# A SwiGLU stage on one core: a corner's sums, the weight sums, the stores and two matmul quarters change places

## The chip, the cores and the metric

The kernel runs on one core of one Trainium2 chip. The metric is the device time of one execution in microseconds (us); lower is better. The core's engines run side by side, each working through its own instructions in order: PE (TensorE, matrix products), DVE (VectorE), ACT (ScalarE), POOL (GpSimd) and SP, which issues transfers (DMA). An engine waits for another by a semaphore, and everything behind the waiting instruction on that engine waits too. Matrix products land in PSUM banks; other data is in SBUF.

## The reference

One transformer block over 1024 tokens of width 1024 in fp32. The change concerns its last part, the feed-forward layer (D_FF is 2816):

```python
h2 = rmsnorm(x, norm2_g[layer])
gate = jnp.einsum('bsd,df->bsf', h2, w_gate[layer])
up = jnp.einsum('bsd,df->bsf', h2, w_up[layer])
x = x + jnp.einsum('bsf,fd->bsd', jax.nn.silu(gate) * up, w_down[layer])
...
return rmsnorm(x, final_g)
```

Ahead of it stand a normed input projection, attention in 8 heads, a pooling mixer and an output projection.

## The kernel before

**Precision.** An fp32 value is split in a high and a low fp32r part (`split`: ACT writes the high part, L120, and DVE the low one, L121). A product of two such values is three matmuls (`mm3`): high by high (L161), page high by block low (L162), page low by block high (L163). A split pair of weight tiles is called a page. Three page slots are used in turn, so page n can be written when the products of page n−3 are done.

**The gate/up stage** runs from about 440 to 853 us over `NG` = 11 pairs of 128-wide blocks of D_FF. Each pair is a 2x2 block product done with seven products instead of eight (Strassen and Winograd's scheme): P1 to P7. Four of them need sums of weight blocks, which POOL makes (`gu_sums`, L1091: s1 to s4; s3 feeds P7, s2 P6, s1 P5, s4 P3). A product is 24 matmuls of 128x512 in two halves, n = 0 and 1. It adds up in PSUM: banks c1 take P1, P6 and P5 one after the other, banks c3 take P7 and then P4. From pair 1 on P3, and from pair 3 (`BOTH`) on P2 as well, is split a second time into seven quarter products Q1 to Q7 of 6 matmuls of 128x256 (`fine_product`), whose results DVE adds to SBUF tiles (L1277). Their pages come in two parts, "a" (Q1, Q2, Q7, Q4) and "b" (Q5, Q3, Q6), and `fine_sums` (DVE, L1234) makes the sums for them in place. In the trace these quarters write to `fineA`, `fineB` and `fineC`.

In pairs 3 to 10 the order is P1, P7, P2 and P6 interleaved, P5, then P3 and P4 interleaved, and the tables `PIECES` and `PIECES2` say how. After P1, P6 and P5 ACT copies c1's banks to SBUF (`snap`, L1153). The four corners of the result are then

- h11: P1's snapshot with P2's quarters added, Silu on ACT (L1302), product on POOL (L1303);
- h22: from c3 after P5 (`corner`: sums on DVE, L1172 and L1174, Silu on ACT, L1173, product on POOL, L1175);
- h21: the same from c3 after P4;
- h12: P5's snapshot with P3's quarters added, Silu on ACT (L1308), product on DVE (L1310).

POOL makes four features f1 to f4 out of these (L1179). Seven tiles a pair, corners and features, are stored to DRAM (`spill`, ACT's queue, L1281).

**The down stage** (to the end) reads them back and multiplies them with the down weights by the same seven-product scheme, in four groups of pairs. `down_sum` (L1349) makes sums of weights, `down_page` splits them, and L1614 adds results.

**Order.** A scheduler places each engine's instructions by priority. Where the code says `tc.issue_after(x)`, the instruction comes behind x on its engine; `mark[...]` remembers the last instruction of a kind (the last matmul, page, high part, quarter add, sum).

Of the kernel before, what the change touches and what calls it, by code (L numbers as in the profile page):

```python
# [30 lines left out]
NG = NF // 2  # L31
# [14 lines left out]
def tile_kernel(  # L46
# [1033 lines left out]
    def gu_sums(j):  # L1080
        a11, a12, a21, a22 = gu_parts(j)
        s1, s2, s3, s4 = (xw_tile(f"s{i}", f"s{i}_{j}", (P, 2, 512)) for i in (1, 2, 3, 4))
        at = None
        todo = [
            (s1, a21, a22, ALU.add), (s2, s1, a11, ALU.subtract), (s3, a11, a21, ALU.subtract), (s4, a12, s2, ALU.subtract)
        ]
        if j >= BOTH:
            todo.insert(0, todo.pop(2))
        for out, in0, in1, op in todo:
            with tc.issue_after(at.ins) if at and j >= BOTH else ExitStack():  # L1090
                at = nc.gpsimd.tensor_tensor(out=out, in0=in0, in1=in1, op=op)  # L1091
# [62 lines left out]

    spills = []
    feats = {}

    def feature(j, name, key):
        t = feats[name] = wk_tile("h", RING, f"{name}_{j}")
        if key:  # L1160
            spills.append((hsd[key, j], t))
        return t

    def corner(j, name, key, src, to):

        h = feature(j, name, to)
        q = wk_tile("q" if key else "e2", 1, f"q{name}_{j}")
        if key is None:
            nc.scalar.activation(out=q, in_=banks[src, 0], func=AF.Silu)
            nc.vector.tensor_tensor(out=h, in0=banks[src, 1], in1=q, op=ALU.mult)  # L1170
        else:
            nc.vector.tensor_tensor(out=q, in0=banks[src, 0], in1=snaps[j, key, 0], op=ALU.add)  # L1172
            nc.scalar.activation(out=q, in_=q, func=AF.Silu)  # L1173
            mark[name, j] = nc.vector.tensor_tensor(out=h, in0=banks[src, 1], in1=snaps[j, key, 1], op=ALU.add)  # L1174
            nc.gpsimd.tensor_tensor(out=h, in0=h, in1=q, op=ALU.mult)  # L1175
# [79 lines left out]
    def fine_product(j, k, q, acc):  # L1255

        at = FINE_BANK[q]
        if q in ("Q1", "Q7", "Q2"):
            own = BANKS["c2", int(k == "P3")], 1
            fine_banks[at] = bank(f"fine{at}_{j}{k}", *(own if at == "C" else ("m", 2)))  # L1260
        ps = fine_banks[at][:, QTR[0]]
        wh, wl = fine[j, k, q]
        bh, bl = fine[BLOCK[k], q]
        for c in range(2):
            ws = slice(c * P, (c + 1) * P)
            mm3(
                ps, wh[:, ws], wl[:, ws], bh[:, c, :], bl[:, c, :],
                q in ("Q1", "Q7", "Q2") and c == 0, q in ("Q3", "Q4", "Q2") and c == 1, True,
            )
        n, h = FINE_TO[q]  # L1270
        out = acc[n][:, QTR[h]]
        with ExitStack() as order:
            if q != "Q1":
                order.enter_context(tc.issue_after(mark["add"].ins))
            if (k, q) == ("P2", "Q3"):
                order.enter_context(tc.issue_after(mark["page"].ins))
            mark["add"] = nc.vector.tensor_tensor(out=out, in0=ps, in1=out, op=ALU.add)  # L1277

    def spill(due, q=nc.scalar):
        for d, h in due:  # L1280
            q.dma_start(out=d, in_=h)  # L1281

    def h22_from(j):
        return "P5" if j else "P7"

    def after(j, k):
        if k in ("P1", "P6", "P5"):
            with tc.issue_after(mark["P3a"][1].ins) if k == "P5" and j >= BOTH else ExitStack():
# [10 lines left out]
        if k == "P2b":  # L1299
            acc = [snaps[j, "sP1", n] for n in range(2)]  # L1300
            with tc.issue_after(mark["hi"].ins):
                nc.scalar.activation(out=acc[0], in_=acc[0], func=AF.Silu)  # L1302
            nc.gpsimd.tensor_tensor(out=acc[1], in0=acc[1], in1=acc[0], op=ALU.mult)  # L1303
            feats["h11"] = acc[1]
            spills.append((hsd["P1", j], acc[1]))
        if k == "P3b":
            acc = [snaps[j, "sU4", n] for n in range(2)]
            nc.scalar.activation(out=acc[0], in_=acc[0], func=AF.Silu)  # L1308
# [3 lines left out]
        if k == ("P3b" if j else "P4"):  # L1312
            with tc.issue_after(mark["add"].ins) if j else ExitStack():
                corner(j, "h21", "sU2", "c3", "P2")
        if k in ("P3", "P3b"):
            feature_sum(j, "f1", "P5", "h12", "h22", ALU.add)
            feature_sum(j, "f2", "P6", "f1", "h11", ALU.subtract)
            feature_sum(j, "f3", "P7", "h11", "h12", ALU.subtract)
        if k == ("P3b" if j else "P4"):
# [6 lines left out]
    PAGES = (("t3h", "t3l", "t1h", "t1l"), ("b22h", "b22l", "t4h", "t4l"))  # L1326
    SUMS = dict(P5="t2h", P6="t2l", P7="b21h", P4="b21l")
# [17 lines left out]
    def down_sum(b, k):  # L1345
        a0, a1 = dict(P5=("b12", "P1"), P6=("P3", "P5"), P7=("P3", "b12"), P4=("P2", "P6"))[k]
        t = blk_tile(SUMS[k], [P, len(GROUPS[b]), 512], F32, f"sum{k}_{b}")
        eng = nc.gpsimd if (b, k) in ((0, "P7"), (0, "P4")) else nc.vector
        eng.tensor_tensor(out=t, in0=moving[b, a0], in1=moving[b, a1], op=ALU.subtract)  # L1349
        moving[b, k] = t  # L1350

# [32 lines left out]
    WINDOWS2 = {"P2a": (0, "P2", "P6"), "P6": (1, "P2", "P6"), "P2b": (2, "P2", "P6")}  # L1384
    WINDOWS3 = {"P3a": (0, "P3", "P4"), "P4": (1, "P3", "P4"), "P3b": (2, "P3", "P4")}
    window = {j: dict(WINDOWS3 if j else {}, **(WINDOWS2 if j >= BOTH else {})) for j in range(NG)}

    def next_page(j, k):
        if (j, k) not in pages:
# [4 lines left out]
        if j + 1 < NG:  # L1394
# [3 lines left out]
                gu_raw(j + 1, 1)  # L1398
            if k == ("P3b" if j else "P4"):
                operands[j + 1] = gu_sums(j + 1)  # L1400

    PACE = {(1, "P1"): 3, (1, "P2"): 3, (2, "P1"): 2, (2, "P2"): 2, (2, "P6"): 3, (2, "P7"): 3}
    waiting = []
    for i, (j, k) in enumerate(todo):
        if i + 2 < len(todo) and (j < BOTH or k != "P1"):
            with ExitStack() as order:
                if j >= BOTH and k == "P3b":
                    order.enter_context(tc.issue_after(mark["add"].ins))
# [10 lines left out]
                mark["P3a"] = mark["page"], mark["hi"]  # L1419
        waiting.append(spills[:])  # L1420
        spills.clear()
        while len(waiting) > (1 if j < BOTH else 3):
            with tc.issue_after(mark["hi"].ins):
                spill(waiting.pop(0))
        if i == 1:
            product(j, k, 0, (0, 1))
            with tc.issue_after(mark["turn", ORDER[-1]].ins):
# [58 lines left out]
    for tt in range(NT):  # L1486
        nc.sync.dma_start(out=x2[tt], in_=x2d[tt])
# [171 lines left out]
```

## Time and profile before

| | us |
| --- | --- |
| median of 3 runs (1078.88 to 1079.73) | 1079.56 |
| the profiled execution | 1080.41 |
| its span in the trace | 1078.6 |
| PE busy | 1032.6 |
| DVE, ACT, POOL busy | 766.0, 470.0, 403.4 |
| granted clock of PE, mean over the span | 0.994 of full |

PE is busy 96% of the span. A row of the timeline gives start, duration, engine, line, operation and output<-inputs; in brackets stands how long the engine sat idle before it and whose work ended that. Rows of the list of waits give the total, the number of times and the longest.

### The profile page before, as it was taken

To read this page: it belongs to the slowest core of one execution; us is meant where nothing else is said; L and a number is where in the kernel's file an instruction comes from. 1 tells how busy PE (TensorE), PEld (TensorE's weight loads), DVE (VectorE), ACT (ScalarE), POOL (GpSimd) and SP (SyncE) were. 2 spreads that over 40 slices of the span, in tenths; PEclk is the share of its full clock that TensorE was granted. 3 is DMA by queue.
4 is the path that set the end of the run, shared out by engine and by line. 5 is a ranking of instruction groups with operands and counts; after the bars stand their busy time and mean duration, and the time that the engine had idled before them with its cause. 6 is when DMAs were issued, how large, how long until landed. Compare 5 with 4: busy or idle time off the path is not lost. (4 is left out here: it accounts for less than half of the span.)

```text
span 1078.6 us, 15149 instructions
## 1 busy us (share of the span) xinstructions
PE 1032.6 (96%) x5428; PEld 881.0 (82%) x5428; DVE 766.0 (71%) x1224; ACT 470.0 (44%) x759; POOL 403.4 (37%) x316
## 2 busy tenths in 40 slices
PE   9999999999999999998898998998998989999997
PEld 8988888998888888887787787887887868888886
DVE  7465566676885598988657657556566789888787
ACT  7343465565673375334234233332333323433345
POOL 4440121223461150846443734734735430000035
PEclk9999999999999999999999999999999989999999
DMA  6224334144831352323042142142146763344424
GB/s 240 51 69 138 79 102 111 42 114 118 299 107 31 110 167 60 127 83 113 11 147 90 57 147 88 59 146 88 59 127 201 251 221 126 138 166 156 147 88 156
DMA packets 108859, 130.28 MB, mean 121 GB/s; under 512 B 8040, under 2 KB 71024, under 8 KB 108784
## 3 DMA queue, kind: packets, MB, share of 16 engines
q1 hardware_dynamic: 97216, 108.18, 32.1%
q10 hardware_dynamic: 10928, 19.42, 5.0%
q0 software_dynamic: 640, 1.71, 0.5%
q8 instruction: 43, 0.70, 0.3%
q14 instruction: 32, 0.26, 0.1%
HBM read 86.29 MB, written 33.03 MB: 111 GB/s over the span
## 5 line engine op out<-in xcount | busy, mean ns | idle before, releaser
L162 PE MATMUL d<-d,d 128*128 128x512 f32 (+1 forms) x308 | 120.9, 393 | 4.0 <-DVE d L121 4.0
L163 PE MATMUL d<-d,d 128*128 128x512 f32 (+1 forms) x308 | 120.2, 392 | 0.0
L629 POOL TENSOR_SCALAR p<-p,rr 128x128 f32<-128x128 f32 (+3 forms) x64 | 48.7, 766 | 177.1 <-DVE rr L628 130.7
L161 PE MATMUL d<-d,d 128*128 128x512 f32 x308 | 109.7, 392 | 0.9 <-ACT d L120 0.7
L120 ACT ACTIVATE d<-r_f 128x1536 fp32r<-128x1536 f32 (+1 forms) x28 | 38.7, 1383 | 116.9 <-PE d L162 115.7
L162 PEld LDWEIGHTS d<-d,d 128*128 128x128 f32 x308 | 58.6, 190 | 16.6 <-DVE d L121 4.5
L161 PEld LDWEIGHTS d<-d,d 128*128 128x128 f32 x308 | 58.1, 189 | 14.2 <-ACT d L120 1.7
L163 PEld LDWEIGHTS d<-d,d 128*128 128x128 f32 x308 | 58.7, 191 | 12.1
L1510 POOL TENSOR_SCALAR sse<-sse 128x1 f32<-128x1 f32 x7 | 3.5, 497 | 171.4 <-ACT junk L1506 171.2
L1175 POOL TENSOR_TENSOR h<-h,qh 128x512 f32<-128x512 f32 x25 | 47.5, 1899 | 45.0 <-ACT qh L1173 39.2
L626 ACT ACTIVATE p<-p,mn 128x128 f32<-128x128 f32 (+3 forms) x64 | 49.4, 773 | 32.2 <-DVE mn L620 29.4
L121 DVE TENSOR_TENSOR gu_P_l<-s,gu_P_h 128x1024 fp32r<-128x1024 f32 (+1 forms) x38 | 53.9, 1428 | 6.7 <-ACT gu_P_h L120 6.6
L648 DVE TENSOR_TENSOR tl<-tp,th 128x512 fp32r<-128x512 f32 (+1 forms) x80 | 49.5, 633 | 9.8 <-ACT th L647 8.8
L120 ACT ACTIVATE gu_P_h<-s 128x1024 fp32r<-128x1024 f32 (+1 forms) x38 | 36.5, 968 | 42.0 <-PE gu_P L162 33.4
L1614 DVE TENSOR_TENSOR x2f_s<-d,x2f_s 128x512 f32<-128x512 f32 x64 | 42.8, 685 | 13.6 <-PE d L163 13.6
L121 DVE TENSOR_TENSOR d<-r_f,d 128x1536 fp32r<-128x1536 f32 (+1 forms) x28 | 46.0, 1644 | 6.8 <-ACT d L120 6.8
L163 PE MATMUL qk<-hTh,l_qk 128*128 128x512 f32 x128 | 50.7, 396 | 0.0
L161 PE MATMUL qk<-hTh,h_qk 128*128 128x512 f32 x128 | 50.6, 395 | 0.0
L162 PE MATMUL qk<-hTl,h_qk 128*128 128x512 f32 x128 | 50.4, 394 | 0.0
L647 ACT ACTIVATE th<-tp 128x512 fp32r<-128x512 f32 (+1 forms) x80 | 42.4, 550 | 15.6 <-PE tp L643 12.7
L1153 ACT ACTIVATE sn_sU<-gu_P 128x512 f32<-128x512 f32 x44 | 26.0, 590 | 50.6 <-PE gu_P L163 25.0
L1303 POOL TENSOR_TENSOR sn_sP<-sn_sP,sn_sP 128x512 f32<-128x512 f32 x8 | 11.4, 1421 | 96.8 <-ACT sn_sP L1302 96.8
(1174 smaller groups left out, 3389.6 us busy)
## 6 DMA issues: line engine op xcount, KB each, us to landing
r_f<-hsdP SPq DMA_DIRECT2D x77, 256.0 KB
r<-in_w_gate_dram SPq DMA_DIRECT2D x44, 256.0 KB
r<-in_w_up_dram SPq DMA_DIRECT2D x44, 256.0 KB
r_wd<-in_w_down_dram SPq DMA_DIRECT2D x22, 512.0 KB
hsdP<-f ACTq DMA_DIRECT2D x40, 256.0 KB
s<-hi SPq DMA_DIRECT2D x64, 128.0 KB
hsdP<-h ACTq DMA_DIRECT2D x23, 256.0 KB
x<-in_x_dram SPq DMA_DIRECT2D x8, 512.0 KB
```

Source lines behind the costliest of these rows:

```text
L120: mark["hi"] = nc.scalar.activation(out=hi, in_=src, func=AF.Copy)
L121: return eng.tensor_tensor(out=lo, in0=src, in1=f32(hi), op=ALU.subtract)
L161: nc.tensor.matmul(ps, lh, rh, start=start, stop=False, **kw)
L162: nc.tensor.matmul(ps, lh, rl, start=False, stop=False, **kw)
L163: mark["mm"] = nc.tensor.matmul(ps, ll, rh, start=False, stop=stop, **kw)
L626: nc.scalar.activation(out=pr[:, :n], in_=pr[:, :n], func=AF.Exp, scale=-1.0, bias=mn, accum_out=rs)
L629: nc.gpsimd.tensor_scalar(out=pr[:, :n], in0=pr[:, :n], scalar1=rr, scalar2=1.0, op0=ALU.mult, op1=ALU.mult)
L647: nc.scalar.activation(out=th[:, :w], in_=tp[:, :w], func=AF.Copy)
L648: nc.vector.tensor_tensor(out=tl[:, :w], in0=tp[:, :w], in1=f32(th[:, :w]), op=ALU.subtract)
L1153: mark["snap"] = nc.scalar.activation(out=t, in_=banks["c1", n], func=AF.Copy)
L1175: nc.gpsimd.tensor_tensor(out=h, in0=h, in1=q, op=ALU.mult)
L1614: added = nc.vector.tensor_tensor(out=row, in0=ps, in1=row, op=ALU.add)
```

## The change

Nothing computed changes, except where a tile lies; the edits change who does what, and when.

1. **Second corner behind the fourth product.** h21's two sums on DVE move from behind Q3 of P3 to behind Q6's add, where P4 ends. Its first sum goes back into the snapshot `sU2` it reads instead of the tile `q`. Its product on POOL stands behind s4.
2. **Weight sums ahead.** POOL's order is s3, s1, s2, s4, then h22's and h21's products, then f1 to f4; h22's product was between s3 and s1. The features and h12 are written down at the next pair's P1.
3. **Quarters between halves.** Behind P4, Q5 of P3 comes at once, then half 0 of the next pair's P1, Q3, and half 1; before, 10 matmuls of P1 stood ahead of Q5 and the other 14 between Q5 and Q3. Whole products follow each other in the order of the program, so in pair 2 P6 comes ahead of P7. P2's part "b" sums are made early, and on DVE all three stand ahead of the quarter adds.
4. **Stores spread.** Of the seven stores of a pair, two (h11, h22) were issued together with P1's end of the next pair and five after P6's page; now two go at the next pair's P7, two at P3a (h21, f1), two at P4 (f2, f3) and one at P3b (f4).
5. **Start of down.** Group 0's four sums of weights all go to POOL in pair 10 (before, two on DVE at the transition, two on POOL), and the tiles for pages and sums trade places. h11's store in pair 10 goes by POOL's queue.

POOL at the boundary of pairs 6 and 7, before (`s_7` are sums of pair 7, `r_7` its raw weights, `h_6` and `f_6` corners and features of pair 6, `qh` and `sU` the factors):

```order
L1091 TENSOR_TENSOR s_7_7095<-r_7_7029,r_7_7050 128x1024
L1175 TENSOR_TENSOR h_6_7083<-h_6_7083,qh_6_7084 128x512
L1091 TENSOR_TENSOR s_7_7093<-r_7_7050 128x1024
L1091 TENSOR_TENSOR s_7_7094<-s_7_7093,r_7_7029 128x1024
L1091 TENSOR_TENSOR s_7_7096<-r_7_7029,s_7_7094 128x1024
L1175 TENSOR_TENSOR h_6_7188<-h_6_7188,qh_6_7189 128x512
L1179 TENSOR_TENSOR f_6_7194<-sn_sU_7081,h_6_7083 128x512
L1179 TENSOR_TENSOR f_6_7196<-f_6_7194,sn_sP_6898 128x512
```

and after:

```order
L1091 TENSOR_TENSOR s_7_7085<-r_7_7020,r_7_7053 128x1024
L1091 TENSOR_TENSOR s_7_7083<-r_7_7053 128x1024
L1091 TENSOR_TENSOR s_7_7084<-s_7_7083,r_7_7020 128x1024
L1091 TENSOR_TENSOR s_7_7086<-r_7_7020,s_7_7084 128x1024
L1181 TENSOR_TENSOR h_6_7074<-h_6_7074,qh_6_7075 128x512
L1181 TENSOR_TENSOR h_6_7169<-h_6_7169,sn_sU_7012 128x512
L1190 TENSOR_TENSOR f_6_7199<-sn_sU_7072,h_6_7074 128x512
L1190 TENSOR_TENSOR f_6_7200<-f_6_7199,sn_sP_6897 128x512
```

Behind s3 h22's product has gone from its place ahead of s1 to one behind s4, next to h21's.

DVE at the same place, before (`fineA_6P` is the bank of Q5 and Q3, `gu_P_6909` and `gu_P_6922` the two c3 banks):

```order
L1277 TENSOR_TENSOR sn_sU_7081<-fineA_6P_7101,sn_sU_7081 128x256 x2
L121 TENSOR_TENSOR gu_P_l<-s_7_7095,gu_P_h 128x1024
L1234 TENSOR_TENSOR r_7_7029<-r_7_7029 128x256
L1277 TENSOR_TENSOR sn_sU_7079<-fineA_6P_7101,sn_sU_7079 128x256
L1172 TENSOR_TENSOR qh_6_7189<-gu_P_6909,sn_sU_7021 128x512
L1174 TENSOR_TENSOR h_6_7188<-gu_P_6922,sn_sU_7023 128x512
L1310 TENSOR_TENSOR sn_sU_7081<-sn_sU_7081,sn_sU_7079 128x512
L121 TENSOR_TENSOR gu_P2a_l<-r_7_7029,gu_P2a_h 128x1024
L121 TENSOR_TENSOR gu_P_l<-s_7_7094,gu_P_h 128x1024
```

and after:

```order
L1288 TENSOR_TENSOR sn_sU_7072<-fineA_6P_7094,sn_sU_7072 128x256
L1178 TENSOR_TENSOR sn_sU_7012<-gu_P_6905,sn_sU_7012 128x512
L1180 TENSOR_TENSOR h_6_7169<-gu_P_6918,sn_sU_7014 128x512
L1288 TENSOR_TENSOR sn_sU_7072<-fineA_6P_7094,sn_sU_7072 128x256
L121 TENSOR_TENSOR gu_P_l<-s_7_7085,gu_P_h 128x1024
L1288 TENSOR_TENSOR sn_sU_7070<-fineA_6P_7094,sn_sU_7070 128x256
L1245 TENSOR_TENSOR r_7_7020<-r_7_7020 128x256
L1340 TENSOR_TENSOR sn_sU_7072<-sn_sU_7072,sn_sU_7070 128x512
L121 TENSOR_TENSOR gu_P2a_l<-r_7_7020,gu_P2a_h 128x1024
L1245 TENSOR_TENSOR r_7_7020<-r_7_7020 128x256
L121 TENSOR_TENSOR gu_P_l<-s_7_7084,gu_P_h 128x1024
L1245 TENSOR_TENSOR r_7_7020<-r_7_7020 128x256 x2
```

The two reads of c3, which stood behind the sum on `r_7` and Q3's add, now stand ahead of Q5's last add; the three sums on `r_7` are woven between the low pages.

ACT's stores, pair 7's tiles, before:

```order
L120 ACTIVATE gu_P2b_h<-r_8_7362 128x768
L120 ACTIVATE gu_P_h<-s_8_7426 128x1024
L1281 DMA hsdP_7_4839<-h_7_7521 128x512
L1281 DMA hsdP_7_4872<-f_7_7527 128x512
L1281 DMA hsdP_7_4850<-f_7_7529 128x512
L1281 DMA hsdP_7_4861<-f_7_7531 128x512
L1281 DMA hsdP_7_4883<-f_7_7533 128x512
L1153 ACTIVATE sn_sU_7687<-gu_P_7536 128x512
L120 ACTIVATE gu_P3a_h<-s_8_7429 128x1024
```

and after:

```order
L120 ACTIVATE gu_P3b_h<-s_8_7418 128x768
L1292 DMA hsdP_7_4839<-h_7_7501 128x512
L1154 ACTIVATE sn_sU_7736<-gu_P_7535 128x512
L1292 DMA hsdP_7_4872<-f_7_7531 128x512
L120 ACTIVATE gu_P_h<-r_9_7684 128x1024
L1292 DMA hsdP_7_4850<-f_7_7532 128x512
L1292 DMA hsdP_7_4861<-f_7_7533 128x512
L1179 ACTIVATE sn_sU_7676<-sn_sU_7676 128x512
```

One row of four features and h21 in a line has become single stores between high pages and snapshots.

The core of the diff:

```diff
@@ gu_sums
                 at = nc.gpsimd.tensor_tensor(out=out, in0=in0, in1=in1, op=op)
+        mark["s4"] = at
@@ corner
-        q = wk_tile("q" if key else "e2", 1, f"q{name}_{j}")
+        if key == "sU2" and j >= BOTH - 1:
+            q = snaps[j, key, 0]
+        else:
+            q = wk_tile("q" if key else "e2", 1, f"q{name}_{j}")
...
-            nc.gpsimd.tensor_tensor(out=h, in0=h, in1=q, op=ALU.mult)
+            done = lambda: nc.gpsimd.tensor_tensor(out=h, in0=h, in1=q, op=ALU.mult)
+            if name == "h22" and BOTH <= j < NG - 1:
+                pending.append(done)
+            else:
+                with tc.issue_after(mark["s4"].ins) if name == "h21" and j >= BOTH - 1 else ExitStack():
+                    done()
@@ after
-        if k == "P3b":
...
+        if k == h21_from(j):
+            with tc.issue_after(mark["Q6" if k == "P4" else "add"].ins) if j else ExitStack():
+                corner(j, "h21", "sU2", "c3", "P2")
+        if k == "P3b" and BOTH - 1 <= j < NG - 1:
+            for name in ("f1", "f2", "f3", "f4"):
+                ready[name] = wk_tile("h", RING, f"{name}_{j}")
+        elif k in ("P3", "P3b"):
+            features(j)
@@ down_sum
-        eng = nc.gpsimd if (b, k) in ((0, "P7"), (0, "P4")) else nc.vector
+        eng = nc.vector if b else nc.gpsimd
@@ tables and the loop over products
+    NEXT = {"P2b": (("P5", 0), "Q3"), "P5": (("P5", 1),), "P3b": (("P1", 0), "Q3"), "P1": (("P1", 1),)}
...
+        if j >= BOTH and k == "P2a":
+            fine_sums(j, "P2", "b")
...
-        while len(waiting) > (1 if j < BOTH else 3):
+        elif k in ("P7", "P3a", "P4", "P3b"):
+            rest = sum(waiting, [])
+            due = [e for e in rest if e[1] < j and (k != "P7" or e[0] in ("P1", "P4"))][: 8 if k == "P3b" else 2]
+            waiting[:] = [[e for e in rest if e not in due]]
             with tc.issue_after(mark["hi"].ins):
-                spill(waiting.pop(0))
+                spill(due)
...
+            deep = j >= BOTH and (j, little) != (NG - 1, "P3") or (j, k) == (BOTH - 1, "P3b")
+            for piece in NEXT[k] if deep and k in NEXT else (PIECES2 if deep else PIECES)[step]:
...
             for n in range(2):
-                product(j, k, n)
+                with tc.issue_after(mark["mm"].ins) if j >= BOTH or j == BOTH - 1 and k != "P1" else ExitStack():
+                    product(j, k, n)
...
-        if j >= BOTH and k == "P1":
-            with tc.issue_after(mark["snap"].ins):
-                next_page(*todo[i + 2])
@@ behind the loop
-        lows = down_page(1)
-    with tc.issue_after(lows[1].ins):
-        for key in ("P5", "P6"):
-            down_sum(0, key)
+        down_page(1)
...
-    for k in ("P7", "P4"):
-        down_sum(0, k)
```

More of the change, by code (lines that the diff above doesn't have):

```diff
@@ L1276, in fine_product @@
                 order.enter_context(tc.issue_after(mark["page"].ins))
-            mark["add"] = nc.vector.tensor_tensor(out=out, in0=ps, in1=out, op=ALU.add)
+            mark["add"] = mark[q] = nc.vector.tensor_tensor(out=out, in0=ps, in1=out, op=ALU.add)
     def spill(due, q=nc.scalar):
-        for d, h in due:
-            q.dma_start(out=d, in_=h)
+        for key, j, h in due:
+            q.dma_start(out=hsd[key, j], in_=h)
     def h22_from(j):
@@ L1304, in after, with h21_from, features @@
             feats["h11"] = acc[1]
-            spills.append((hsd["P1", j], acc[1]))
-        if k == "P3b":
+            spills.append(("P1", j, acc[1]))
+        if k == h21_from(j):
[6 more added lines that the diff above has]
+            features(j)
+        if j == 0 and k == "P4":
+            feature_sum(j, "f4", "P3", "h21", "f2", ALU.subtract)
+    def h21_from(j):
+        return "P4" if j == 0 or j >= BOTH - 1 else "P3b"
+    def features(j, *behind):
+        if j:
             acc = [snaps[j, "sU4", n] for n in range(2)]
-            nc.scalar.activation(out=acc[0], in_=acc[0], func=AF.Silu)
+            with ExitStack() as order:
+                for ins in behind:
+                    order.enter_context(tc.issue_after(ins.ins))
+                nc.scalar.activation(out=acc[0], in_=acc[0], func=AF.Silu)
             with tc.issue_after(mark["page"].ins):
@@ L1311, in after @@
             feats["h12"] = acc[1]
[L1312 to L1319, printed above, removed]
+        feature_sum(j, "f1", "P5", "h12", "h22", ALU.add)
+        feature_sum(j, "f2", "P6", "f1", "h11", ALU.subtract)
+        feature_sum(j, "f3", "P7", "h11", "h12", ALU.subtract)
+        if j:
             feature_sum(j, "f4", "P3", "h21", "f2", ALU.subtract)
@@ L1325, in tile_kernel @@
     BANK3 = (("m", 2), ("m", 2), ("tp1", 1), ("po", 1))
-    PAGES = (("t3h", "t3l", "t1h", "t1l"), ("b22h", "b22l", "t4h", "t4l"))
-    SUMS = dict(P5="t2h", P6="t2l", P7="b21h", P4="b21l")
+    PAGES = (("b21h", "b21l", "t1h", "t1l"), ("b22h", "b22l", "t4h", "t4l"))
+    SUMS = dict(P5="t3h", P6="t3l", P7="t2h", P4="t2l")
     steps2 = [(b, k) for b in range(len(GROUPS)) for k in ORDER2]
@@ L1431, in tile_kernel @@
             step, little, whole = window[j][k]
-            acc = [snaps[j, dict(P2="sP1", P3="sU4")[little], n] for n in range(2)]
-            for piece in (PIECES2 if j >= BOTH else PIECES)[step]:
+            acc = [snaps.get((j, dict(P2="sP1", P3="sU4")[little], n)) for n in range(2)]
+            deep = j >= BOTH and (j, little) != (NG - 1, "P3") or (j, k) == (BOTH - 1, "P3b")
+            for piece in NEXT[k] if deep and k in NEXT else (PIECES2 if deep else PIECES)[step]:
                 with tc.issue_after(mark["mm"].ins):
@@ L1444, in tile_kernel @@
         else:
+            if j >= BOTH and k == "P1":
+                features(j - 1)
+                with tc.issue_after(mark["add"].ins), tc.issue_after(mark["h21", j - 1].ins):
+                    next_page(*todo[i + 2])
             after(j, k)
-        if j >= BOTH and k == "P1":
-            with tc.issue_after(mark["snap"].ins):
-                next_page(*todo[i + 2])
         if j == NG - 1:
@@ L1455, in tile_kernel @@
                     down_load(par)
+            if k == "P2b":
+                for key in ("P5", "P6", "P7", "P4"):
+                    down_sum(0, key)
             if k == "P3a":
@@ L1466, in tile_kernel @@
         for _ in range(min(PACE.get((j, k), 2 if j < 2 else 0), len(finer))):
-            with tc.issue_after((mark["page"] if j else mark["h22", 0]).ins):
+            with tc.issue_after((shown if j == 2 else mark["page"] if j else mark["h22", 0]).ins):
                 finer.pop(0)()
```

27 lines of the change are left out of this document (22 added, 5 removed).

## The prediction

> **What bounds the kernel now.** I read the busy times by stretch first, then PE's (TensorE's) waits, then the timeline of one pair boundary.
>
> ```profile
> 485.00:524.00 39.00, 32.63 (x150) 26.40 (x149) 29.75 (x33) 13.33 (x19) 22.85 (x11) 0.96 0.26 88
> 524.00:848.00 324.00, 299.54 (x1604) 254.79 (x1603) 200.74 (x283) 113.74 (x152) 173.21 (x86) 1.00 0.34 110
> 848.00:882.00 34.00, 28.54 (x114) 22.20 (x114) 28.88 (x31) 9.30 (x10) 13.98 (x11) 0.90 0.67 227
> ```
>
> The columns after the length are PE, PEld, DVE, ACT and POOL busy, the granted clock, and DMA. PE is the bound throughout, so what the change can win is PE's idle time: 6.37 us in pair 2 (485 to 524), 24.46 us in pairs 3 to 10, 5.46 us where the down stage begins. The diff touches nothing after 882. Who ends these waits:
>
> ```profile
> PE gu_P L161 <- ACT sn_sU L1308: 11.0, 7, 1.7
> PE d L162 <- DVE d L121: 4.0, 1, 4.0
> PE fineA_2P L161 <- DVE sn_sU L1277: 2.7, 1, 2.7
> PE gu_P L161 <- ACT sn_sU L1153: 2.5, 3, 1.1
> PE gu_P L163 <- DVE gu_P_l L121: 2.2, 1, 2.2
> PE fineB_4P L161 <- DVE sn_sP L1277: 1.5, 1, 1.5
> ...
> PE fineB_3P L161 <- DVE sn_sP L1277: 1.1, 1, 1.1
> ```
>
> (us in total, times, longest.) The first row is P7 waiting in 7 pairs. The fineB rows are quarter Q4 of P2, one for each of pairs 3 to 10, 11.1 us for the eight. Here is the pair boundary 6/7:
>
> ```profile
> 684.32 0.39 PE L163 MATMUL gu_P<-t4h,gu_P_l 128*128 128x512 f32 x1
> 691.21 0.28 PE L162 MATMUL fineA_6P<-b22l,gu_P3b_h 128*128 128x256 f32 x1
> 691.33 0.28 PE L163 MATMUL fineA_6P<-b22h,gu_P3b_l 128*128 128x256 f32 x1
> 693.08 0.47 PE L161 MATMUL gu_P<-t3h,gu_P_h 128*128 128x512 f32 x1 [1.47 <-ACT sn_sU L1308]
> 681.11 2.27 POOL L1175 TENSOR_TENSOR h<-h,qh 128x512 f32<-128x512 f32 x1
> 688.28 3.26 POOL L1091 TENSOR_TENSOR s<-r,s 128x1024 f32<-128x1024 f32 x1
> 691.58 0.43 DVE L1234 TENSOR_TENSOR r<-r 128x256 f32<-128x256 f32 x1 [2.29 <-POOL s L1091]
> 692.25 0.68 DVE L1172 TENSOR_TENSOR qh<-gu_P,sn_sU 128x512 f32<-128x512 f32 x1
> 692.85 0.68 DVE L1174 TENSOR_TENSOR h<-gu_P,sn_sU 128x512 f32<-128x512 f32 x1
> ```
>
> P7 writes the c3 banks that P4 filled. P4's last matmul is done at 684.7, but DVE reads them for the corner h21 (L1172, L1174) only at 692.25. ACT's L1308 is named since it ended last by the profile; it doesn't touch those banks. What holds P7 is L1172, which ends at 692.93 behind a sum (L1234) that waited for POOL's s4. The two rows before P7 show what a gap costs beyond its listed idle: fine matmuls follow 0.12 us apart, so P7 was due at 691.45 and came 1.63 later, 0.16 over the listed 1.47. I take 0.2 a gap.
>
> **P7's wait.** The corner's two adds move behind Q6's add. They then run right at P4's end, 684.7 to 686.0, 5.5 us before P7 is due. Q5 and Q3 only change places among P1's matmuls, so nothing new is computed. Gain 11.0 + 7 x 0.2 = 12.4. What queues behind the adds on DVE is Q5's add and P7's low page; both have 5 us.
>
> **Q4 of P2.** It waits for Q7's add on DVE:
>
> ```profile
> 694.52 1.06 ACT L120 ACTIVATE gu_P2a_h<-r 128x1024 fp32r<-128x1024 f32 x1
> 695.62 2.01 DVE L121 TENSOR_TENSOR gu_P2a_l<-r,gu_P2a_h 128x1024 fp32r<-128x1024 f32 x1 [1.49 <-ACT gu_P2a_h L120]
> 697.55 2.30 DVE L121 TENSOR_TENSOR gu_P_l<-s,gu_P_h 128x1024 fp32r<-128x1024 f32 x1
> 699.77 1.51 DVE L1234 TENSOR_TENSOR r<-r 128x256 f32<-128x256 f32 x1
> 701.54 1.51 DVE L1234 TENSOR_TENSOR r<-r 128x256 f32<-128x256 f32 x2
> 703.31 0.41 DVE L1277 TENSOR_TENSOR sn_sP<-fineB_7P,sn_sP 128x256 f32<-128x256 f32 x1
> 703.77 0.38 PE L161 MATMUL fineB_7P<-b21h,gu_P2a_h 128*128 128x256 f32 x1 [1.44 <-DVE sn_sP L1277]
> 696.62 2.15 POOL L1179 TENSOR_TENSOR f<-f,sn_sP 128x512 f32<-128x512 f32 x1
> ```
>
> After the change POOL does s1, s2, s4 ahead of h22's product, so s4 ends 2.27 earlier, at 689.3. The sum after it takes 0.4, ACT's high page 1.06, h12's step on DVE lies between (0.7, the size of L1174), and P2a's low page can begin near 692.0 instead of 695.62. From there I keep the slow durations of before, since f1 to f4 run beside it again: 2.0, 1.5, 2.3, 1.5, then the three adds of 0.35 each: 692.0 + 7.3 + 1.05 gives Q7's add done at 700.3. Q4 was due at 703.77 − 1.44 = 702.3, and P7 now begins 1.63 earlier, so it is due at 700.7. The margin is 0.4 us, small beside these estimates: between no wait and the whole 1.4 I take 0.4 left a pair. Gain 11.1 + 8 x 0.2 − 8 x 0.4 = 9.5.
>
> [...]
>
> **Stores.** ACT issued four of them at once:
>
> ```profile
> 664.23 4.09 ACTq L1281 DMA_DIRECT2D hsdP<-f  x4
> 668.37 0.60 ACT L1153 ACTIVATE sn_sU<-gu_P 128x512 f32<-128x512 f32 x1 [3.58 <-PE gu_P L162]
> ```
>
> The snapshot of P6 came behind them and P5 waited in two of the later pairs (2.5 less pair 2's 1.1 = 1.4). Two at a time hold ACT for about 2.0 by the first row, on an engine that is 35% busy (113.74 of 324). One now stands ahead of the second P5 snapshot: 0 to 1.0 a pair; I take nothing, as that snapshot is followed by a low page on DVE that bounds Q7 anyway. Gain 1.4 + 2 x 0.2 = 1.8.
>
> **Pair 2 and the start of down.** The PE clock fell to half after two stalls:
>
> ```profile
> 688.06 1.22 DVE L121 TENSOR_TENSOR gu_P_l<-s,gu_P_h 128x1024 fp32r<-128x1024 f32 x1
> 519.20:522.70 3.50, 3.50 (x10) 0.51 0.00 0
> 872.10:877.50 5.40, 5.40 (x14) 0.50 0.82 252
> 871.64 0.79 PE L162 MATMUL d<-d,d 128*128 128x512 f32 x1 [4.03 <-DVE d L121]
> 866.97 4.62 DVE L121 TENSOR_TENSOR d<-sumP,d 128x1024 fp32r<-128x1024 f32 x1
> 866.91 2.36 POOL L1349 TENSOR_TENSOR sumP<-r_wd,sumP 128x1024 f32<-128x1024 f32 x1
> ```
>
> The first is behind the 2.7 us wait of fineA_2P (Q5 of pair 2), the second behind the 4.0. Of 3.50 us at 0.51 about 1.7 is lost, of 5.40 at 0.50 2.7. No slow stretch follows the 2.2 us wait or the P7 waits.
>
> Pair 2: Q5 now stands directly behind P4 and P3's adds, and the sum that held its bank's release stands behind it, so the 2.7 and the lost 1.7 go; h21 goes early and P7 follows P6, so the 2.2 and 1.1 go. New: P6 behind P2 needs P1's snapshots, which ACT does behind two high pages: two pages of 1.06 less cover, 0 to 2.1; I take 1.8. Gain 6.37 + 1.7 − 1.8 = 6.3.
>
> Start of down: all four sums of group 0 go to POOL in pair 10, 4 x 2.36 = 9.4 us that its idle half covers (173 of 324 busy). They leave the transition, so the low page of 4.62 has only f1 to f3 beside it. It then takes between 1.22 (a page of its size with POOL idle) and 3.4 (a POOL instruction of 2.15 in its way); I take 2.2, nearer the page of 2.30 beside f2, so it is 2.4 shorter and 1.6 of the 4.0 stay. Gain 5.46 + 2.7 + 3 x 0.2 − 1.6 = 7.2.
>
> **Sum.** 12.4 + 9.5 + 1.8 + 6.3 + 7.2 = 37.2 us. The profiled execution took 1080.41, 0.85 over the median of the runs: 1080.41 − 37.2 = 1043.2, or 1042.4 as a median. I forecast 1042. With none of the leftovers (3.2 + 1.8 + 1.6) it would be 1036; with a residue of 0.9 at each Q4 and 2 more at the transition, 1048. Its own range is 1036 to 1048.
>
> [...]
>
> **Rivals.**
> - Q4 stays late (0.15): the low pages and sums on DVE slide under POOL's f1 to f4, which start earlier too. Q7's add then comes at 702 and Q4 waits 1.4 as before: 1042 + 9.5 = 1052. For it: 2.01, 2.30 and 1.51 beside POOL against 1.22 and 0.43 without. Against it: f1 to f4 end 2 us earlier too.
> - The transition or pair 2 keeps its stall with the half clock (0.12): the sums move, but the page of 4.62 still sits beside f1 to f3 and a stall over 2.7 trips the clock: 1042 + 7 = 1049.
> - New waits in each pair (0.08): a store on ACT waits for h22's product, which now stands behind s4, and ACT's snapshots of P1 wait behind the store. P6 begins six of its matmuls ahead of Q4, near 699, and the snapshots end near 693, so it bites once s4 is over 6 us late, or a store is; at 2 us a pair, 8 pairs, 1058.
> - Slower (0.04): the weight sums come late because the loads do.
>
> ```profile
> r<-in_w_gate_dram SPq DMA_DIRECT2D x44, 256.0 KB
> hsdP<-f ACTq DMA_DIRECT2D x40, 256.0 KB
> 675.08 0.37 SPq L1048 DMA_DIRECT2D r<-in_w_gate_dram  x1
> 678.75 2.41 POOL L1091 TENSOR_TENSOR s<-r,r 128x1024 f32<-128x1024 f32 x1 [2.53 <-DMA r<-in_w_up_dram]
> ```
>
>   Two stores, each as large as a load, are now issued near 676, among four loads that take 3.7 us to s3's start. Six for four would be 5.5, 1.8 later. The slack is 2.0 at least: P2a's low page ended at 697.63 before and kept nobody waiting, which is 696.0 with P7 1.63 earlier, against 694.0 now. To lose the whole 37 us the eight pairs must each lose 4.7, so it decides from s4 being 6.7 us late; at 7.3 late the time is 1085. DMA is 34% busy in this stretch, which speaks against it.
> - The change doesn't do what it says, or its gain is eaten to within 0.2%, which is about what a measurement tells from no change (0.03): 1079.
>
> The forecast keeps 0.58. Range: from 1034, a little under the forecast with no leftovers, up to 1057, which takes in Q4, the transition and most of the new waits. Faster by over 0.2% 0.92, within 0.2% 0.03, slower 0.05.
>
> **What the next profile would show.** Right: no P7 wait in the list (none above 0.3); fineB rows of pairs 3 to 10 under 0.5; the granted clock 1.00 in pair 2; PE idle in 524 to 848 of a few us; the first d wait under 2. Wrong: P7 waiting for the page of s3 or a snapshot; fineB rows at 1.4 still; an ACT snapshot ended by a store; a P2a page that waits for POOL past PE's need.

## The result, and the profile after

The changed kernel took 1068.28 us in the median (1060.33 to 1069.82), the kernel before 1079.22: a ratio of 0.9884, interval 0.9835 to 0.9933. It is faster by 11 us; I had forecast 37. The profiled execution took 1069.82 with a span of 1068.0.

The same stretches as before (PE, PEld, DVE, ACT, POOL busy, granted clock, DMA):

```profile
485.00:524.00 39.00, 37.16 (x177) 31.00 (x176) 29.63 (x37) 14.91 (x23) 24.67 (x13) 0.96 0.28 92
524.00:848.00 324.00, 302.40 (x1581) 257.94 (x1580) 243.78 (x282) 112.98 (x151) 180.00 (x89) 0.96 0.32 106
848.00:882.00 34.00, 34.00 (x157) 28.18 (x156) 32.89 (x39) 12.98 (x14) 10.48 (x10) 1.00 0.85 323
```

PE's idle time went from 6.37 to 1.84 in the first stretch and from 5.46 to nothing in the third. In the middle it only went from 24.46 to 21.6, and there the granted clock fell from 1.00 to 0.96; in the first stretch it is 0.96 as before. The waits of PE:

```profile
PE fineB_5P L161 <- DVE sn_sP L1288: 2.8, 1, 2.8
...
PE fineB_9P L161 <- DVE sn_sP L1288: 2.8, 1, 2.8
PE gu_P L161 <- ACT sn_sP L1154: 1.8, 1, 1.8
PE fineB_3P L161 <- DVE sn_sP L1288: 1.8, 1, 1.8
```

P7's 11.0 us, P5's, the 2.7 in pair 2 and the 4.0 of down are gone. Q4 of P2, 1.4 a pair before, now waits 2.8 in each of pairs 4 to 10. Where that leaves the time can be read from Q4 itself: pair 3's began at 537.92 before and 533.03 now, pair 10's at 828.09 before and 828.04 now. The forecast of the middle row is that of P7, Q4 and the stores, for all eight pairs.

| stretch | before | after | gain | forecast |
| --- | --- | --- | --- | --- |
| start to Q4 of pair 3 | 537.9 | 533.0 | 4.9 | 6.3 |
| Q4 of pair 3 to Q4 of pair 10 | 290.2 | 295.0 | −4.8 | 23.7 |
| Q4 of pair 10 to the end | 250.5 | 240.0 | 10.5 | 7.2 |

So in this profile the seven pairs at the heart of the change got slower, by 0.7 us each. A part of that is the clock. Where it stays at 1.00 a pair takes 40.8 us from Q4 to Q4, and 42.2 to 43.3 where it falls; before, a pair took 41.0 to 42.2, in the mean 41.5. Behind Q4 of pair 6, and behind the wait of 1.8 in pair 2 (P6, which starts at 488.01), PE ran at half clock (PE busy, granted clock, DMA):

```profile
660.00:662.00 2.00, 2.00 (x8) 0.50 0.15 40
490.00:492.00 2.00, 2.00 (x6) 0.50 0.02 7
```

Here is pair 6/7 after, one row for each place that matters (PE, SP's issue of the loads, POOL, DVE):

```profile
659.45 0.47 PE L161 MATMUL fineB_6P<-b21h,gu_P2a_h 128*128 128x256 f32 x1 [2.81 <-DVE sn_sP L1288]
672.07 1.23 DVE L121 TENSOR_TENSOR gu_P_l<-r,gu_P_h 128x1024 fp32r<-128x1024 f32 x1
673.32 0.37 SPq L1048 DMA_DIRECT2D r<-in_w_gate_dram  x1
678.05 2.41 POOL L1091 TENSOR_TENSOR s<-r,r 128x1024 f32<-128x1024 f32 x1 [3.60 <-DMA r<-in_w_up_dram]
680.42 3.39 POOL L1091 TENSOR_TENSOR s<-r 128x1024 f32<-128x1024 f32 x1
686.36 3.26 POOL L1091 TENSOR_TENSOR s<-r,s 128x1024 f32<-128x1024 f32 x1
689.65 1.50 DVE L1245 TENSOR_TENSOR r<-r 128x256 f32<-128x256 f32 x1 [1.96 <-POOL s L1091]
691.07 1.78 DVE L1340 TENSOR_TENSOR sn_sU<-sn_sU,sn_sU 128x512 f32<-128x512 f32 x1
695.35 2.31 DVE L121 TENSOR_TENSOR gu_P_l<-s,gu_P_h 128x1024 fp32r<-128x1024 f32 x1
697.58 2.91 DVE L1245 TENSOR_TENSOR r<-r 128x256 f32<-128x256 f32 x2
701.27 0.41 DVE L1288 TENSOR_TENSOR sn_sP<-fineB_7P,sn_sP 128x256 f32<-128x256 f32 x1
689.72 0.39 PE L161 MATMUL gu_P<-t3h,gu_P_h 128*128 128x512 f32 x1
698.51 0.39 PE L163 MATMUL gu_P<-t2h,gu_P_l 128*128 128x512 f32 x1
701.74 0.39 PE L161 MATMUL fineB_7P<-b21h,gu_P2a_h 128*128 128x256 f32 x1 [2.84 <-DVE sn_sP L1288]
```

P7 starts at 689.72 with no wait. The sixth matmul of P6 starts at 698.51, and Q4 stands still until Q7's add at 701.27 is done. Read from top to bottom, the rows but those of P7 (689.72) and P6 (698.51) are one closed chain. Q4 of pair 6 lets PE go on to P5. Behind P5's first half DVE makes P4's low page (672.07), which is the last to read that tile of raw weights; it ends at 673.30, and SP issues the next pair's loads (673.32). The loads release s3 (678.05), POOL's four sums end with s4 (689.62), DVE makes pages and sums and adds Q7, and only then does Q4 of pair 7 start. Each pair's chain starts from the Q4 of the pair before, so it is a loop, and its length is the time of a pair. For before, its start is

```profile
662.77 0.39 PE L161 MATMUL fineB_6P<-b21h,gu_P2a_h 128*128 128x256 f32 x1 [1.44 <-DVE sn_sP L1277]
```

and the other rows are in the prediction:

| part of the loop | before | after |
| --- | --- | --- |
| Q4 to the first load's issue | 662.77 to 675.08: 12.31 | 659.45 to 673.32: 13.87 |
| load, to s3's start | 678.75: 3.67 | 678.05: 4.73 |
| POOL, to the end of s4 | 691.54: 12.79 | 689.62: 11.57 |
| DVE, to Q4 | 703.77: 12.23 | 701.74: 12.12 |
| sum | 41.00 | 42.29 |

The first part is 1.6 longer after because PE runs a part of it at half clock: with the clock at 1.00 it is 12.31 in the changed kernel too (e10 below). PE's own work in a pair is 37.6 us (37.59 in e2 below, where PE never waits in these pairs). It was idle before because this loop is longer, in two places, ahead of P7 and at Q4. With P7's place freed, all of the idle time gathers at Q4.

### The profile page after: what moved, and what is told of

The parts are those of the page before. It is cut to its first block, busy times and chain, and to the rows that moved or that the text cites. A ratio compares the mean times of both kernels' runs of the same rounds, so it can differ in the third digit from the quotient of the medians.

```text
span 1068.0 us, 15171 instructions
## 1 busy us (share of the span) xinstructions
PE 1035.7 (97%) x5428; PEld 886.4 (83%) x5428; DVE 804.0 (75%) x1222; ACT 470.6 (44%) x759; POOL 408.5 (38%) x319
## 4 chain that ended last, share of the span: by engine, by line
PE 77%; DVE 8%; POOL 5%; issue 4%; DMA 3%; ACT 1%; SPq 0%; POOLq 0%; ACTq 0%; DVEq 0%
PE d L161 6%; PE d L163 6%; PE d L162 6%; PE gu_P L161 6%; PE gu_P L162 6%; PE gu_P L163 6%; POOL s L1091 4%; PE po L657 3%; PE tp L643 3%; PE qk L162 3%; PE qk L161 3%; PE qk L163 3%; PE o L162 3%; PE o L163 3%; PE o L161 3%
## 5 line engine op out<-in xcount | busy, mean ns | idle before, releaser
L162 PE MATMUL d<-d,d 128*128 128x512 f32 (+1 forms) x308 | 119.2, 388 | 0.0
L163 PE MATMUL d<-d,d 128*128 128x512 f32 (+1 forms) x308 | 119.0, 388 | 0.0
L121 DVE TENSOR_TENSOR gu_P_l<-s,gu_P_h 128x1024 fp32r<-128x1024 f32 (+1 forms) x38 | 70.3, 1862 | 6.3 <-ACT gu_P_h L120 6.0
L1245 DVE TENSOR_TENSOR r<-r 128x256 f32<-128x256 f32 x32 | 45.4, 1437 | 15.8 <-POOL s L1091 15.5
L1314 POOL TENSOR_TENSOR sn_sP<-sn_sP,sn_sP 128x512 f32<-128x512 f32 x8 | 10.5, 1306 | 108.9 <-ACT sn_sP L1313 108.9
L121 DVE TENSOR_TENSOR gu_P_l<-r,gu_P_h 128x1024 fp32r<-128x1024 f32 x24 | 42.7, 1783 | 7.8 <-ACT gu_P_h L120 4.6
L620 DVE CUSTOM_DVE_ANT_0 p<-z,wmask 128x128 f32<-128x128 f32 (+3 forms) x64 | 33.7, 535 | 13.6 <-PE z L618 9.7
```

Of the source, the lines that this page charges most:

```text
L121: return eng.tensor_tensor(out=lo, in0=src, in1=f32(hi), op=ALU.subtract)
L162: nc.tensor.matmul(ps, lh, rl, start=False, stop=False, **kw)
L163: mark["mm"] = nc.tensor.matmul(ps, ll, rh, start=False, stop=stop, **kw)
L1245: mark["sum"] = nc.vector.tensor_tensor(out=out, in0=in0, in1=in1, op=op)
```

## The experiments

Two theories stood against each other. **Sum theory**, the prediction's: each wait is worth its own length. **Loop theory**: the loop above sets the time of a pair; a wait that is removed inside it comes back further on, and only what shortens the loop pays, down to PE's own 37.6 us.

**e1: the corner alone, on the kernel before.**

```diff
+        if key == "sU2" and j >= BOTH:
+            q = snaps[j, key, 0]
...
-        if k == ("P3b" if j else "P4"):
-            with tc.issue_after(mark["add"].ins) if j else ExitStack():
+        if k == ("P4" if j == 0 or j >= BOTH else "P3b"):
+            with tc.issue_after(mark["Q6" if j >= BOTH else "add"].ins) if j else ExitStack():
                 corner(j, "h21", "sU2", "c3", "P2")
+        if k == "P3b" and late_mult:
+            with tc.issue_after(mark["s4"].ins):
+                late_mult.pop(0)()
```

> The kernel before with one part of the change alone: h21's two sums right behind P4, its first sum kept in the snapshot, its product on POOL still behind s4 (pairs 3 to 10). Sum theory (each wait counts by itself, as the prediction had it): P7's 11.0 us go and Q4's stay, so 1079 - 12 = 1067. Loop theory (one circle sets the period: P4's page frees the raw weights' tile, load, POOL's sums, DVE's pages, Q7's add, Q4, and back to P4's page): P7's wait turns up again at Q4, which waits about 1.4 + 1.6 = 3 us instead of 1.4; the time stays at 1076 to 1080, or goes up to 1088 where stalls near 3 us put the clock to half.

Measured: 1081.11, ratio 1.0016 (0.9999 to 1.0032). From its waits of PE and its timeline:

```profile
PE fineB_8P L161 <- DVE sn_sP L1285: 4.1, 1, 4.1
PE fineB_7P L161 <- DVE sn_sP L1285: 2.5, 1, 2.5
PE d L162 <- DVE d L121: 1.1, 2, 0.8
659.70 0.58 PE L161 MATMUL fineB_6P<-b21h,gu_P2a_h 128*128 128x256 f32 x1 [2.50 <-DVE sn_sP L1285]
701.95 0.38 PE L161 MATMUL fineB_7P<-b21h,gu_P2a_h 128*128 128x256 f32 x1 [2.52 <-DVE sn_sP L1285]
607.00:649.00 42.00, 39.39 (x215) 1.00 0.30 95
```

There is no P7 wait any more, and no time is won. Q4 waits 2.5 to 4.1 instead of 1.4 in pairs 4 to 10, and this pair takes 42.25 (659.70 to 701.95). Its clock is 0.96; the pair ahead of it, at a clock of 1.00 (last row), takes 40.77 (618.93 to 659.70), against 41.5 in the mean before. So at full clock less than half of P7's 1.6 a pair is won, and the half clock behind the longer stalls takes it back. Most of the 11 us that the list of waits showed at P7 were not there to be had. The last wait of the list is a by-product: the 4.0 us at down's start are 1.1 here, though nothing was changed there.

**e2: the features behind Q7's add, on the changed kernel.**

```diff
             if j >= BOTH and k == "P1":
-                features(j - 1)
...
                 if (k, piece) == ("P2a", "Q7"):
                     with tc.issue_after(mark["Q7"].ins):
                         next_page(j, "P2b")
+                    features(j - 1)
```

> The changed kernel with h12's product on DVE moved behind Q7's add and P2b's low page; f1 to f4 on POOL need h12, so they can't run beside P2's and P6's low pages and sums any more. If POOL beside DVE is what makes Q4 late: P6's low page 2.3 to 1.2, the two sums 2.9 to 0.8, the single sum 1.4 to 0.4, h12's 1.8 out of the way; Q7's add comes some 4.5 us earlier, Q4's wait of 2.8 is gone, the clock stays full, and a pair takes PE's own 37.7 us instead of 42.1: 1036, at most 1044. If the weight sums alone set Q4: Q4 still waits 2 or more and the time is 1060 to 1068.

Measured: 1038.60 (1037.21 to 1040.72), ratio 0.9627 (0.9608 to 0.9645). Five instructions a pair later on their engines, and 30 us less. DVE, POOL, SP and a stretch of its trace (columns as in the windows: PE busy, clock, DMA):

```profile
673.39 0.43 DVE L1245 TENSOR_TENSOR r<-r 128x256 f32<-128x256 f32 x1
673.73 1.22 DVE L121 TENSOR_TENSOR gu_P_l<-s,gu_P_h 128x1024 fp32r<-128x1024 f32 x1
674.87 0.76 DVE L1245 TENSOR_TENSOR r<-r 128x256 f32<-128x256 f32 x2
677.44 0.42 DVE L1288 TENSOR_TENSOR sn_sP<-fineB_7P,sn_sP 128x256 f32<-128x256 f32 x1 [0.35 <-PE fineB_7P L163]
679.47 1.31 POOL L1190 TENSOR_TENSOR f<-sn_sU,h 128x512 f32<-128x512 f32 x1 [7.39 <-issue]
653.19 0.37 SPq L1048 DMA_DIRECT2D r<-in_w_gate_dram  x1
690.78 0.37 SPq L1048 DMA_DIRECT2D r<-in_w_gate_dram  x1
607.00:649.00 42.00, 42.00 (x228) 1.00 0.33 107
```

The sum that took 1.40 takes 0.43, P6's low page 1.22 instead of 2.31, the two sums together 0.76 instead of 2.91. These three alone are 4.2 us. s4 to the end of Q7's add is 8.46 instead of 12.06 (669.40 to 677.86): h12's step of 1.78 has left this part too, but DVE now waits 1.2 there for ACT's high page and 1.0 for PE's quarters. No run moves h12 alone. From one load to the next it is 37.59, PE is busy without a gap, and the clock stays at 1.00. POOL is idle beside these three (7.39 us ahead of 679.47) and had its features there in the changed kernel; why DVE's rows are longer beside POOL's, no run shows. The adds that read PSUM take 0.41 to 0.43 in both kernels.

**e3: no store beside the loads.** On the changed kernel, `elif k in ("P7", "P3a", "P4", "P3b")` loses `"P3a"`.

> The changed kernel with no store in P3a: h21 and f1 go at P4, the other three at P3b, so none is issued beside the four loads of weights. If the stores slow these loads (4.7 us from the first issue to s3 against 3.7 before): load back to 3.7, Q4 waits 1.8 instead of 2.8, 8 us less and more where the clock then stays full: 1050 to 1060. If not: 4.7 and 2.8 stay, 1068.

Measured: 1062.20 (1061.19 to 1064.01), ratio 0.9845 (0.9828 to 0.9863).

```profile
669.89 0.37 SPq L1048 DMA_DIRECT2D r<-in_w_gate_dram  x1
673.58 2.41 POOL L1091 TENSOR_TENSOR s<-r,r 128x1024 f32<-128x1024 f32 x1 [2.56 <-DMA r<-in_w_up_dram]
697.30 0.39 PE L161 MATMUL fineB_7P<-b21h,gu_P2a_h 128*128 128x256 f32 x1 [1.87 <-DVE sn_sP L1288]
607.00:649.00 42.00, 39.94 (x208) 0.96 0.29 95
```

The load is back to 3.69, and Q4 waits 1.9 here (1.6 to 2.3 in pairs 3 to 10). So the two stores cost the loads about 1.0 us, which I had put at up to 1.8 and inside the slack. The time is 2 us over my range; the clock fell here too, to 0.96 in most pairs.

**e4: h22's product ahead of s3.** On the changed kernel, `pending.append(done)` becomes `done()`; POOL then takes it while it waits for the load.

> The changed kernel with h22's product on POOL ahead of s3, in the time in which POOL waits for the load, instead of behind s4. Loop theory: s4 ends as before, and the sum behind it on DVE has no h22 product beside it (1.5 to 0.4), so Q4 waits 1.7 to 2 instead of 2.8: 1050 to 1062. If h22's product delays s3 it is no gain: 1068 or more.

Measured: 1064.47 (1062.67 to 1067.21), ratio 0.9867 (0.9843 to 0.9891).

```profile
673.32 1.30 POOL L1181 TENSOR_TENSOR h<-h,qh 128x512 f32<-128x512 f32 x1 [2.03 <-DVE h L1180]
686.73 1.50 DVE L1245 TENSOR_TENSOR r<-r 128x256 f32<-128x256 f32 x1 [1.96 <-POOL s L1091]
688.15 0.68 DVE L1340 TENSOR_TENSOR sn_sU<-sn_sU,sn_sU 128x512 f32<-128x512 f32 x1
```

The product hides ahead of s3, and h12's step takes 0.68 instead of 1.78. The first sum still takes 1.50, as h21's product has moved into the place beside it. DVE's part of the loop is 0.85 shorter, and Q4 waits 1.7 to 2.3, but 4.2 in pair 10; slightly less was won than I expected.

**e10: PE kept busy while it waits.** 20 extra matmuls ahead of Q4, on the changed kernel:

```diff
+                    if (k, piece) == ("P2a", "Q4"):
+                        wb = bank(f"warm_{j}", BANKS["c2", 1], 1)
+                        for _ in range(20):
+                            mark["mm"] = nc.tensor.matmul(wb[:, QTR[0]], ..., start=True, stop=True)
```

> The changed kernel with 20 extra matmuls of 128x256 ahead of Q4 of P2 in pairs 3 to 10, into a PSUM bank that nobody reads: PE is busy for 2.4 of the 2.8 us that it waits there; the wait itself is as long. If the idle time is what puts PE's clock to half behind Q4: the granted clock stays at 1.00 in these pairs, a pair takes about 40.5 instead of 42.1 us, and the time is 1056 to 1060, with runs closer together. If the clock has another cause: 1066 to 1070, as the changed kernel.

Measured: 1063.12 (1061.91 to 1064.00), ratio 0.9851 (0.9835 to 0.9868).

```profile
698.21 0.39 PE L161 MATMUL fineB_7P<-b21h,gu_P2a_h 128*128 128x256 f32 x1 [0.48 <-DVE sn_sP L1288]
607.00:649.00 42.00, 41.55 (x231) 1.00 0.29 95
```

The clock is 1.00 in each of seven windows from 524 to 817 (0.92 to 1.00 in e11), with PE idle for 0.5 at Q4 instead of 2.8: once the idle time is filled, the half clock is gone. A pair takes 40.85 (657.36 to 698.21): 12.31 + 4.83 + 11.57 + 12.14 by the parts of the loop, as long as the changed kernel's own pairs at full clock (40.8). Work that computes nothing made the kernel 4.5 us faster than e11, on the same chip. That is less than I expected, since the changed kernel has full clock in some of its pairs.

**e11: the changed kernel once more.**

> The changed kernel once more, for the spread of its runs and a second profile. If the half clock alone tells its runs apart: the waits at Q4 are 2.8 us again in each of pairs 4 to 10, runs lie between 1059 and 1071, and the time goes down as the mean granted clock goes up, 1060 at 0.997 and 1070 at 0.986.

Measured: 1067.59 (1064.98 to 1068.75), ratio 0.9888 (0.9870 to 0.9906).

```profile
607.00:649.00 42.00, 39.20 (x205) 0.96 0.29 95
649.00:691.00 42.00, 39.16 (x211) 1.00 0.29 94
```

The waits are 2.8 again in pairs 4 to 10, and PE is busy for the same 39.2 us of 42, but one pair has 0.96 and the next 1.00, and two others have 0.92. Which pairs are hit differs from run to run: this profile has a mean clock of 0.989, the first 0.986, and the run of 1060.33 had 0.997. That is the spread of the changed kernel's runs.

**Undoing parts of the change in the fast version.** e5 puts h21's sums back behind Q3 (part 1), e7 the four sums of down where they were (part 5).

> e2_features_late with part 1 of the change undone in pairs 3 to 9: h21's two sums go back behind Q3's add. If part 1 is what frees P7: P7 waits again, some 1 to 1.5 us in each pair, and the time is 1046 to 1052. If Q3's place between the halves of P1 is enough (its add ends about 2 us ahead of P7, time for two sums of 0.68): no P7 wait and 1037 to 1041, as e2.

> e2_features_late with part 5 undone: group 0's four sums of the down weights where they were (two on DVE, two on POOL, at the start of down). By the prediction's term the wait of about 4 us at the first products of down and its half clock come back, 5 to 8 us: 1044 to 1047. In exchange pair 10 has no sums beside its pages and loses its 1.9 us wait, so 1042 is possible. If part 5 had no share: 1038.

e5: 1038.47 (1038.13 to 1039.23), ratio 0.9624 (0.9608 to 0.9639). No P7 wait. Q3's add, now between P1's halves, is done at 669.10, the two sums end at 670.31, and P7 of pair 7 starts at 671.09. The early corner isn't needed in this version.

e7: 1036.71 (1035.98 to 1037.33), ratio 0.9606 (0.9591 to 0.9621), the fastest of all; pair 10's waits, 1.9 and 0.4 in e2, are gone with the sums. From its waits and timeline:

```profile
PE d L162 <- DVE d L121: 1.7, 2, 1.1
827.50 1.72 DVE L121 TENSOR_TENSOR d<-sumP,d 128x1024 fp32r<-128x1024 f32 x1
828.66 2.82 POOL L1375 TENSOR_TENSOR sumP<-r_wd,sumP 128x1024 f32<-128x1024 f32 x1
```

The 4.0 us don't come back with the sums; 1.7 do, in two waits. Before, the page on DVE and POOL's sum began together (866.97 and 866.91); here 1.2 of the page's 1.7 us are over when the sum begins. Part 5 was not what removed most of that wait; no run isolates what moved the two apart.

**e8 and e9: other places for the sums of down.** e8 puts two behind pair 9's features and two behind h21's product of pair 10; e9 also takes the stores out of P3a.

> e2_features_late with the four sums of part 5 moved on POOL behind the features of pair 9 (two) and behind h21's product of pair 10 (two), so that they lie beside fewer pages and sums of pair 10 on DVE. If POOL's sums make DVE late there, the waits of 1.9 and 0.4 us in pair 10 and the half clock behind them go: 1035 to 1037. If not, or if the later sums delay the down pages by as much: 1038 to 1040.

> e8_two_sums_later with no store in P3a (as in e3). With Q4 off the circle the load has 1.8 us or more to spare, so the loads get faster (4.6 to 3.7) and the time does not: 1035 to 1038, as e8. If the load still bounded a pair, 3 to 8 us less.

e8: 1039.78 (1038.61 to 1041.51), ratio 0.9641 (0.9625 to 0.9657). e9: 1039.98 (1039.13 to 1040.69), ratio 0.9636 (0.9620 to 0.9652), 2 over its range. Nothing won: pair 10's waits shrink to 0.5, and e8's first row of waits is now

```profile
PE d L162 <- DVE d L121: 3.0, 1, 3.0
```

The faster loads of e9 (3.69 from the first issue to s3, as in e3; 4.72 in e8) bring nothing either, as expected off the loop.

**e12: the features late, on the kernel before.** The edit of e2, with h12's product behind Q7's add:

```diff
+                if (k, piece) == ("P2a", "Q7"):
+                    with tc.issue_after(mark["Q7"].ins):
+                        features(j - 1)
```

> The kernel before with the edit of e2 alone: in pairs 2 to 9 h12's product on DVE goes behind Q7's add of the next pair, and f1 to f4 on POOL follow it; the scheduler then also puts h22's product ahead of s3 and the three sums for P2 in a row. Loop theory: the pages and sums on DVE run at their short durations (1.2 instead of 2.0 to 2.3, 0.4 instead of 1.5), so Q4's wait of 1.4 goes; without h22's product between the sums s4 ends 1 to 2 us earlier, and the P7 wait of 1.5 goes for the most part. A pair takes 37.7 to 38.7 instead of 41.5 us; pair 2 and the start of down stay as before: 1052 to 1062. If the corner's place were what holds P7 whatever else is done: P7 keeps its 1.5 us and the time is 1064 to 1068.

Measured: 1083.39 (1083.12 to 1085.36), ratio 1.0044 (1.0027 to 1.0060), a clear miss of mine.

```profile
697.42 1.22 DVE L121 TENSOR_TENSOR gu_P_l<-s,gu_P_h 128x1024 fp32r<-128x1024 f32 x1
677.82 0.37 SPq L1048 DMA_DIRECT2D r<-in_w_gate_dram  x1
682.83 2.40 POOL L1091 TENSOR_TENSOR s<-r,r 128x1024 f32<-128x1024 f32 x1 [0.77 <-DMA hsdP<-f]
695.92 0.47 PE L161 MATMUL gu_P<-t3h,gu_P_h 128*128 128x512 f32 x1 [1.88 <-DVE qh L1173]
```

The low pages are short (1.22) and Q4 of P2 waits no more, as expected; a quarter of P3 waits 1.5 instead (679.11). But the loop closes through P7 now: P7 of pair 6 at 654.52, load issued at 677.82 (P4's page has slipped behind Q1 of P3 in the scheduler's new order), s3 5.0 later with four features' stores beside the loads, s4 done at 694.38, corner, P7 at 695.92. That is 41.4, as long as before. Taking DVE's crowding away from the kernel before isn't enough. By this trace it is the orders that the change fixes, for PE, P4's page and the stores, that let e2 work; no run takes them one by one, so this is argued and not shown.

## Why the prediction was wrong

**P7's wait (12.4).** It vanished as forecast. Counting it whole was an error: e1 shows that alone it wins no time, and less than half of itself at full clock, since P7 and Q4 wait on one loop.

**Q4 of P2 (9.5).** This is the step that failed: Q7's add was forecast 0.4 ahead of Q4 and came 2.8 behind it. Measured from the first load's issue, Q4 was due at 25.6 us (701.74 less the wait of 2.84), as I had it. Q7's add was forecast at 25.2 (700.3 less 675.08) and came at 28.4 (701.68). Of the 3.1 us, 1.06 is the load, slowed by the two stores that I priced only in the rival "slower" (e3). I set it there against a slack of 2.0 ahead of P2a's page; but that page is a link of the chain to Q7's add, whose margin was 0.4. 1.05 is POOL's part: it was to fall by the whole 2.27 of h22's product and fell by 1.22 (12.79 to 11.57), s1 taking 3.39 where s3 takes 2.41. And 1.0 is DVE's part: I kept the old durations, 2.0 + 1.5 + 2.3 + 1.5, and had the sum behind s4 at 0.4, h12 at 0.7 and the two last sums at 1.5. They took 1.50, 1.78 and 2.91, the page of P2a 1.21 instead of 2.0. The row of 1.51 for two sums that I went by was a mild case: alone they take 0.76 (e2), wholly beside POOL 2.91. The page of 1.22 at 688.06 that I called one with POOL idle ran beside POOL's sums; the sum beside it, s4, took 3.26 where s3 took 2.41. The rival "Q4 stays late" named what the rows show, longer DVE instructions beside POOL's (2.31 against 1.22 for P6's low page, changed kernel against e2), but stopped at the old wait of 1.4, and its 1052 kept P7's gain whole; a margin of 0.4 should have had it above 0.15.

**The clock.** I wrote that no slow stretch follows P7's waits or the one of 2.2, and the sum had none for what was left. Behind stalls of 1.8 to 2.8 the clock stood at 0.50 in some pairs (490 to 492, 660 to 662). In the profiled run that is a mean clock of 0.96 instead of 1.00 over the middle stretch, some 9 us by its seven pairs (295.0 less 7 x 40.8); e10 prices it at 4 to 5 us against e11. What decides which stall a slow stretch follows is not shown: with equal stalls of 2.8, e11's windows have 0.92, 0.96 and 1.00.

**Pair 2 (6.3) and down (7.2).** Measured 4.9 and 10.5. In pair 2 P6 waits 1.8 for P1's snapshot, as forecast, but the clock falls to half behind it, so the 1.7 that I counted as won there is not; and Q4 of pair 3 waits 1.8 instead of 1.1. At down I left 1.6 of the wait, and none stayed; the 3.4 at which I bounded the low page there added two rows, an estimate that no run shows, and the page took 2.30 (at 860.24) with nobody waiting; a wait of 0.8 at a quarter of P3 in pair 10, which no term had, went too. The credit to part 5 was wrong for the most part: in e1 and e7 most of that wait is gone with the sums where they were.

**Stores (1.8).** P5's wait went, but it is gone in e1 too, where the stores are as before, so the credit to their spreading isn't shown. One of their new places costs the loads 1.0 a pair.

## What to carry to other kernels

Before adding up waits, look for the loop: follow the last wait back through the tile that must come free, and if the chain comes round to the same instruction one iteration earlier, its length is the iteration's time, and only its parts count. When an instruction moves, price it by what runs beside it at the new place, on both engines: here two sums took 2.91 beside POOL's features and 0.76 without. A margin under a microsecond at the end of a dozen such instructions is no margin: 0.4 was forecast here, and Q4 waited 2.8.

## What was unexpected of the hardware

In the changed kernel's profile TensorE's clock stood at 0.50 behind the waits of 1.8 to 2.8 us in pairs 2, 3, 5, 6, 8 and 9 (from 660 to 662 in pair 6), and at 1.00 behind the same 2.8 in pairs 4, 7 and 10 (from 701 to 705 in pair 7). The runs of this kernel spread over 10 us, 1060.33 at a mean clock of 0.997 and 1069.82 at 0.986. In the profile before, between 480 and 860, no low clock followed the waits of 1.1 to 1.7, nor one of 2.2. With two stores of 256 KB beside the four loads of 256 KB, the loads took 4.73 us to s3's start, and 3.69 without them (e3).
